# Rotary tables computed once per angle on folded tiles, softplus pinned in its place, and the swaps of rotary halves issued from GpSimd's queue

## The chip, the core and the metric

The kernel runs on one core of a Trainium2 chip. The core has five engines with a queue of instructions each, taken in order: TensorE (PE) multiplies matrices into PSUM, VectorE (DVE) and ScalarE (ACT) work on tiles in SBUF and PSUM, GpSimd (POOL) is a slower helper, and SyncE (SP) mostly issues DMAs. SP, ACT and POOL can each issue DMAs, and all of them run on the same 16 DMA engines. A tile has 128 partitions and some columns. The metric is the device time of one execution in microseconds, as the median of several runs.

## The reference, cut to what matters

The reference is one layer of an encoder trunk over 256 tokens of width 2048, in float32: a norm, one input projection, multi-head latent attention with rotary position encoding beside a bidirectional state-space branch, a gated mix of the two, an output projection, and a gated MLP with a short convolution. What the change touches is the rotary part of the attention and the softplus of the state-space branch:

```
half = QK_ROPE_DIM // 2                                   # 32
inv_freq = ROPE_THETA ** (-jnp.arange(half) / half)
ang = positions[..., None] * inv_freq
cos, sin = jnp.cos(ang), jnp.sin(ang)
apply_rope: [x1 * cos - x2 * sin, x1 * sin + x2 * cos]    # x1, x2: the halves of 64 columns
dt = softplus(dt_raw + dt_bias)
```

There are 32 frequencies and 256 positions, so 8192 different angles. The rotary part of the 16 heads' queries and the one rotary key are turned by them.

## The kernel before

The work is cut into jobs, each one slab of weights (16 blocks of 128x128, two halves of 8) times the activations of all 256 tokens. A slab arrives by SP's queue as `raw`; `split_to` (L139) splits each half into a high part `wh` (ScalarE, L151) and a low part `wl` (VectorE, L152), in rings of five halves, ahead of the products that use them. Products are made in three or two passes (`mm`, `low` in `dense`; L213 to L215 in `quad`), so that the high and low parts together give float32. The first ten jobs are the latent projections of q and kv (jobs 0 to 7), the rotary key (8) and dt (9); then come the gates, R0 and R1 (jobs 11 and 24, the rotary queries of eight heads each), V and QK, the attention, and after it everything else.

The activations are normalized in `emit_n` (L313 to L315, slots 6 to 8): a product with `r_x` (L311), then a split into high and low parts `xHL` (L290, L291). The jobs from 8 on need them.

Side work is hung on jobs by `at(slot, ...)` (L989): it stands ahead of the products of that job in the program. The rotary tables are a generator, `rope_tables` (L323 to L370), of which `rope_steps` takes 4 steps in each job from 5 on. It loads the positions into all 128 partitions of a 256-column tile by one DMA on ACT's queue (L328). Each partition p has the frequency p % 32, so each angle is computed four times, in partitions 32 apart. A chain of VectorE instructions on 128x256 tiles takes the angle modulo a turn (L337, L338, L341), ScalarE makes two Sins (L366, L367), and three more VectorE instructions make the cosine from the half angle's sine and give the sine its sign (L368 to L370).

`swapped` (L372) copies a tile with neighbouring blocks of 32 partitions exchanged, by four DMAs on ACT's queue: once for the rotary key (L511), twice for each of R0 and R1 (L538). `rotate` (L380) multiplies the swapped tile by `sinT`, the tile by `cosT`, and adds; it runs for the key in slot 14 (`kr_rope`) and for R0 and R1 two slots after their jobs, followed by the splits of L552, L553, L517 and L523.

`dt_softplus` (L443) hangs on job 41, `dt_tokens` (L465), which transposes its results on TensorE, on job 46. Its first instruction, an Exp into `nea` (L445), is pinned by `keep_in_program_order`; the Abs behind it (L447) is not.

Only the first weight splits are in an order written out by hand (`manual_schedule`, L1169). All else is ordered by a planner, which gives each engine its instructions in an order of its own by program order and by when it expects an instruction's inputs. On the chip each engine then keeps to that order, and an instruction whose input is late holds up those behind it.

Tiles named by `p1` share 18 buffers of 128x256; `page` tiles share 29 larger ones; `dr` is a pool in DRAM.

Of the kernel before, what the change touches and what calls it, by code (L numbers as in the profile page):

```python
# [8 lines left out]
F32 = mybir.dt.float32  # L9
F32R = mybir.dt.float32r  # L10
I32 = mybir.dt.int32
AF = mybir.ActivationFunctionType
ALU = mybir.AluOpType
AX = mybir.AxisListType

P = 128
S = 256
# [17 lines left out]
C_ID, C_U, C_L, C_INVF, C_SGN = 0, 128, 256, 384, 385  # L35
# [24 lines left out]
def tile_bidir_hybrid_layer(ctx: ExitStack, tc, xT, pos, vec, cst, w_in, w_r, w_v, w_qk, w_oa,  # L60
                            w_os, w_out, w_up, w_dn, out, RAWB=3, HB=5, NPG=29, NP1=18):
    nc = tc.nc
# [5 lines left out]
    dr = ctx.enter_context(tc.tile_pool(name="dr", bufs=1, space=bass.MemoryType.DRAM))  # L68

    act, dve, pe = nc.scalar, nc.vector, nc.tensor  # L70

    def page(shape, dt=F32, name="pg"):
        return pp.tile(shape, dt, tag="pg", bufs=NPG, name=name)

    def p1(shape=(P, S), dt=F32, name="p1"):
        return pp.tile(list(shape), dt, tag="p1", bufs=NP1, name=name)
# [12 lines left out]
    CT = cp.tile([P, NCONST], F32, name="CT")  # L89
# [13 lines left out]
    def vcol(name, i=0):  # L103
        o = VOFF[name] + i
        return V[:, o:o + 1]
# [213 lines left out]


    rot = {}

    def rope_tables():  # L323

        cosT = rot["c"] = p1(name="cosT")
        sinT = rot["s"] = p1(name="sinT")
        pi_ = p1(dt=I32, name="posi")
        nc.scalar.dma_start(pi_, pos.broadcast_to([P, S]))  # L328
        a = p1(name="ang")
        q = p1(name="angq")  # L330
        qh = p1(name="angqh")
        t = p1(name="angt")
        k = p1(name="angk")
        MAGIC = 12582912.0

        def rounded(dst, src, scale):
            yield dve.tensor_scalar(dst, src, scale, MAGIC, ALU.mult, ALU.add)  # L337
            yield dve.tensor_scalar(dst, dst, MAGIC, None, ALU.subtract)  # L338

        def add_scaled(dst, src, c):  # L340
            yield dve.scalar_tensor_tensor(dst, src, c, dst, ALU.mult, ALU.add)  # L341

        def less_turns():
            yield from rounded(k, a, float(np.float32(1.0 / (2 * np.pi))))
            for c in TURN:
                yield from add_scaled(a, k, -c)


        yield dve.tensor_copy(a, pi_)
        yield dve.tensor_scalar(a, a, CT[:, C_INVF:C_INVF + 1], None, ALU.mult)  # L350
        yield from rounded(q, a, 2.0 ** -12)
        yield from add_scaled(a, q, -2.0 ** 12)
        yield from rounded(qh, q, 2.0 ** -10)
        yield from add_scaled(q, qh, -2.0 ** 10)
        yield dve.tensor_scalar(t, qh, TURN22[0], None, ALU.mult)
        yield from add_scaled(t, q, TURN12[0])
        yield from rounded(k, t, 1.0)
        yield dve.tensor_sub(t, t, k)
        yield from add_scaled(t, q, TURN12[1])
        yield from add_scaled(t, qh, TURN22[1])  # L360
        yield from less_turns()
        yield from add_scaled(a, t, 2 * float(np.pi))
        yield from less_turns()
        lim = float(np.nextafter(np.float32(np.pi), np.float32(0)))
        yield dve.tensor_scalar(a, a, lim, -lim, ALU.min, ALU.max)
        act.activation(sinT, a, AF.Sin)  # L366
        yield act.activation(cosT, a, AF.Sin, scale=0.5)  # L367
        yield dve.tensor_mul(cosT, cosT, cosT)  # L368
        yield dve.tensor_scalar(cosT, cosT, -2.0, 1.0, ALU.mult, ALU.add)
        yield dve.tensor_scalar(sinT, sinT, CT[:, C_SGN:C_SGN + 1], None, ALU.mult)  # L370

    def swapped(q, nb):  # L372

        sw = page([P, nb, S], name="sw")
        for i in range(4):
            o = 32 * (i ^ 1)
            nc.scalar.dma_start(sw[o:o + 32], q[32 * i:32 * i + 32])
        return sw

    def rotate(q, sw, nb):  # L380
# [62 lines left out]
    def dt_softplus():  # L443
        v = dts["v"]
        tc.keep_in_program_order(act.activation(nea, vcol("alog"), AF.Exp))  # L445
        e, t, t2, o = p1(name="e"), p1(name="t"), p1(name="t2"), p1(name="o")
        act.activation(e, v, AF.Abs)  # L447
        act.activation(e, e, AF.Exp, scale=-1.0)
        dve.tensor_scalar(t, e, 2.0, None, ALU.add)
        dve.reciprocal(t, t)  # L450
        dve.tensor_mul(t, t, e)
        dve.tensor_mul(t2, t, t)
        n = 9
        dve.tensor_scalar(o, t2, 2.0 / (2 * n + 1), 2.0 / (2 * n - 1), ALU.mult, ALU.add)
        for k in range(n - 2, -1, -1):
            dve.tensor_mul(o, o, t2)
            dve.tensor_scalar(o, o, 2.0 / (2 * k + 1), None, ALU.add)
        dve.tensor_mul(o, o, t)
        dve.scalar_tensor_tensor(o, v, 0.0, o, ALU.max, ALU.add)
        dts["dt"] = o  # L460
        a = p1(name="a")
        dve.tensor_scalar(a, o, nea, -1.0, ALU.mult, ALU.mult)
        dts["a"] = a
# [44 lines left out]
    def kr_evac(ps):  # L508
        t = p1((P, 1, S), name="krf")
        halves_sum(ps, t[:, 0, :])  # L510
        dts["krf"] = (t, swapped(t, 1))  # L511
# [13 lines left out]
    def r_job(i):  # L525
# [3 lines left out]
        def mm(h, n, wh, wl):  # L529
            ps = gpsum([P, 2, S])  # L530
            cell[h] = ps
            for b in range(2):
                for k in range(4):
                    mm3(ps[:, b, :], wh[:, 4 * b + k, :], wl[:, 4 * b + k, :], hi[:, k, :], lo[:, k, :],
                        k == 0, k == 3)
            t = page([P, 2, S], name="rf")
            act.activation(t, ps, AF.Copy)
            cell["f", h] = (t, swapped(t, 2))  # L538
# [450 lines left out]
    def at(slot, fn, *a):  # L989
        late.append((slot, lambda: fn(*a)))  # L990
# [14 lines left out]
    at(10, lat_norm, "kv")  # L1005
    at(13, lat_norm2, "kv", "kvn")
    steps = rope_tables()

    def rope_steps(n):
        for _ in range(n):  # L1010
            next(steps, None)

    for m in range(5, 14):
        at(m, rope_steps, 4 if m < 13 else 99)
    at(14, kr_rope)
    at(41, dt_softplus)
    at(46, dt_tokens)
    at(48, dt_cumsum)
# [67 lines left out]
    for g in range(G):  # L1086
# [9 lines left out]
        e, f = len(jobs) - b, 1  # L1096
# [205 lines left out]
```

## Time and profile before

| what | value |
|---|---|
| median of 3 runs | 1962.73 us (1962.49 to 1963.57) |
| profiled execution: its own time | 1962.68 us |
| its span, first to last instruction | 1960.9 us |
| TensorE busy | 1945.8 us, 99% |
| VectorE busy | 1444.6 us, 74% |
| ScalarE busy | 1205.3 us, 61% |
| GpSimd busy | 0.2 us, 4 instructions |
| mean granted TensorE clock | 0.998 |
| DMA traffic | 379.31 MB, mean 193 GB/s |

The busy times are of one profiled execution. An engine's busy time is the union of its instructions' spans; instructions overlap at their edges, so what one holds its engine for is read from one start to the next. Matmuls are pipelined, so a busy TensorE is not one at its peak. A wait is put down to the semaphore that came last.

### The profile page before, as it was taken

What the parts mean: (1) busy time and instruction counts of PE and PEld (TensorE: products, weight loads), DVE (VectorE), ACT (ScalarE), POOL (GpSimd) and SP (SyncE); (2) the same over time, 40 slices, a digit from 0 to 9 for tenths busy, and PEclk for the clock granted to TensorE, in tenths of its full rate; (3) what the DMA queues carried; (4) which work ended last, traced back from release to release, by engine and by line L of the source; (5) the groups of instructions that cost most, each with busy time, mean ns of one, the idle gap of its engine ahead of it and who ended that gap; (6) DMA issues with size and microseconds to landing.
All of it is one profiled execution on the core that took longest, in us unless ns stands there. A gap on an engine that the chain in (4) does not pass through costs nothing.

```text
span 1960.9 us, 28920 instructions
## 1 busy us (share of the span) xinstructions
PE 1945.8 (99%) x11136; PEld 1707.2 (87%) x11136; DVE 1444.6 (74%) x2349; ACT 1205.3 (61%) x1878; POOL 0.2 (0%) x4
## 2 busy tenths in 40 slices
PE   9999999999999999999999999999999999999997
PEld 8889988888888888888888888888888888888887
DVE  7897744779779789879755566777656777557775
ACT  6566544687887887978644455666435655346553
POOL 0000000000000000000000000000000000000000
PEclk9999999999999999999999999999999999999999
DMA  7554456765665565565666665555555555555543
GB/s 279 179 173 154 137 172 216 251 222 172 215 233 173 198 234 194 194 215 182 205 196 198 200 222 176 190 193 192 181 189 190 194 192 175 194 192 193 188 161 124
DMA packets 93259, 379.31 MB, mean 193 GB/s; under 512 B 10688, under 2 KB 11328, under 8 KB 62912
## 3 DMA queue, kind: packets, MB, share of 16 engines
q1 hardware_dynamic: 91440, 375.09, 56.6%
q10 hardware_dynamic: 1680, 2.37, 0.4%
q8 instruction: 87, 1.43, 0.3%
q14 instruction: 52, 0.43, 0.1%
HBM read 371.91 MB, written 4.33 MB: 192 GB/s over the span
## 4 chain that ended last, share of the span: by engine, by line
PE 95%; DVE 3%; DMA 1%; ACT 1%; issue 0%; ACTq 0%; DVEq 0%; SPq 0%
PE g L178 42%; PE g L185 22%; PE g L214 7%; PE g L213 7%; PE g L215 7%; PE g L159 1%; PE g L157 1%; PE g L158 1%; DVE wl L152 1%; PE s L789 1%; PE s L798 1%; PE s L158 0%; PE s L159 0%; PE s L157 0%; PE s L771 0%; PE s L634 0%
## 5 line engine op out<-in xcount | busy, mean ns | idle before, releaser
L152 DVE TENSOR_TENSOR wl<-raw,wh 128x1024 fp32r<-128x1024 f32 (+1 forms) x670 | 802.7, 1209 | 328.1 <-ACT wh L151 181.3
L151 ACT ACTIVATE wh<-raw 128x1024 fp32r<-128x1024 f32 (+1 forms) x670 | 698.9, 1047 | 546.6 <-PE g L178 352.0
L178 PE MATMUL g<-xHL,wh 128*128 128x512 f32 x1424 | 341.7, 392 | 1.3 <-DVE xHL L291 1.1
L178 PE MATMUL g<-hHL,wh 128*128 128x512 f32 x1360 | 324.8, 391 | 0.0
L178 PEld LDWEIGHTS g<-xHL,wh 128*128 128x128 f32 x1424 | 262.4, 188 | 53.6 <-DVE xHL L291 1.5
L178 PEld LDWEIGHTS g<-hHL,wh 128*128 128x128 f32 x1360 | 249.8, 188 | 48.3
L185 PEld LDWEIGHTS g<-xHL,wl 128*128 128x128 f32 x1424 | 182.6, 191 | 7.0
L185 PE MATMUL g<-xHL,wl 128*128 128x256 f32 x1424 | 184.9, 283 | 0.0
L185 PEld LDWEIGHTS g<-hHL,wl 128*128 128x128 f32 x1360 | 174.3, 191 | 6.6
L185 PE MATMUL g<-hHL,wl 128*128 128x256 f32 x1360 | 176.4, 283 | 0.0
L178 PE MATMUL g<-aHL,wh 128*128 128x512 f32 x692 | 166.6, 391 | 0.1
L910 DVE SCALAR_TENSOR_TENSOR uc<-u,V,uc 128x255 f32<-128x255 f32 x176 | 85.3, 485 | 88.4 <-ACT uc L908 85.3
L178 PEld LDWEIGHTS g<-aHL,wh 128*128 128x128 f32 x692 | 126.9, 188 | 25.6 <-DVE aHL L928 1.3
L213 PE MATMUL g<-wh,yHL 128*128 128x512 f32 x256 | 100.1, 391 | 0.0
L214 PE MATMUL g<-wl,xHL 128*128 128x512 f32 x256 | 100.0, 391 | 0.0
L213 PE MATMUL g<-wh,xHL 128*128 128x512 f32 x256 | 100.0, 391 | 0.0
L215 PE MATMUL g<-wh,yHL 128*128 128x512 f32 x256 | 99.7, 389 | 0.0
L215 PE MATMUL g<-wh,xHL 128*128 128x512 f32 x256 | 99.6, 389 | 0.0
L214 PE MATMUL g<-wl,yHL 128*128 128x512 f32 x256 | 99.6, 389 | 0.0
L185 PEld LDWEIGHTS g<-aHL,wl 128*128 128x128 f32 x692 | 89.2, 191 | 3.6
L185 PE MATMUL g<-aHL,wl 128*128 128x256 f32 x692 | 90.4, 283 | 0.0
L684 DVE SCALAR_TENSOR_TENSOR xs<-cu,V,xs 128x254 f32<-128x254 f32 (+1 forms) x128 | 59.0, 479 | 0.2
(298 smaller groups left out, 2534.1 us busy)
## 6 DMA issues: line engine op xcount, KB each, us to landing
raw<-in_w_in SPq DMA_DIRECT2D x88, 1024.0 KB, 4.9
raw<-in_w_up SPq DMA_DIRECT2D x88, 1024.0 KB, 4.8
raw<-in_w_in SPq DMA_DIRECT2D x128, 256.0 KB, 3.9
raw<-in_w_os SPq DMA_DIRECT2D x128, 256.0 KB, 3.6
raw<-in_w_dn SPq DMA_DIRECT2D x32, 1024.0 KB, 5.0
raw<-in_w_oa SPq DMA_DIRECT2D x64, 256.0 KB, 3.9
FB<-acsD SPq DMA_DIRECT2D x32, 512.0 KB, 7.4
raw<-in_w_out SPq DMA_DIRECT2D x14, 1024.0 KB, 5.0
```

Source lines behind the costliest of these rows:

```text
L151: act.activation(vh, r, AF.Copy)
L152: dve.tensor_sub(vl, r, f32(vh))
L157: pe.matmul(ps, lhsT=wH, rhs=xH, start=first, stop=False)
L158: pe.matmul(ps, lhsT=wH, rhs=xL, start=False, stop=False)
L159: pe.matmul(ps, lhsT=wL, rhs=xH, start=False, stop=last)
L178: pe.matmul(ps, lhsT=wh[:, b, :], rhs=x, start=k == 0, stop=False)
L185: pe.matmul(cell["ps"][:, 0, :], lhsT=wl[:, b, :], rhs=get(k)[:, 0, :], start=False, stop=k == ktot - 1)
L213: pe.matmul(ps, lhsT=x[:, 0, ts], rhs=wH[:, kk, :], start=k == 0, stop=False)
L214: pe.matmul(ps, lhsT=x[:, 0, ts], rhs=wL[:, kk, :], start=False, stop=False)
L215: pe.matmul(ps, lhsT=x[:, 1, ts], rhs=wH[:, kk, :], start=False, stop=k == kt - 1)
L684: dve.scalar_tensor_tensor(o[:, a], u[:, b], vcol("cw", k * 48 + cb), o[:, a], ALU.mult, ALU.add)
L910: dve.scalar_tensor_tensor(o[:, a], u[:, b], vcol("fcw", k * 88 + cb), o[:, a], ALU.mult, ALU.add)
```

## The change

The positions are loaded folded: partition block c (32 partitions) of a 64-column tile holds positions 64c to 64c+63, by four DMAs on ACT's queue. Each angle is then computed once, on 128x64 tiles, which are slices of one tile `ang`; sine and cosine lie side by side in `tr`. Four DMAs from GpSimd's queue store the pair to DRAM (`rotD`, 32 x 2 x 256), and eight load it back, four for the cosine and four for the sine, each into 32 partitions of a 128x256 tile. The sign is applied after that, on the spread tile. `rope_steps` takes 8 steps in each job from 5 on, not 4. `swapped` issues its DMAs from GpSimd's queue. The Abs of the softplus is pinned to its place in the program.

```
     rot = {}
+    rotD = dr.tile([32, 2, S], F32, name="rotD")
     def rope_tables():
-        cosT = rot["c"] = p1(name="cosT")
-        sinT = rot["s"] = p1(name="sinT")
-        pi_ = p1(dt=I32, name="posi")
-        nc.scalar.dma_start(pi_, pos.broadcast_to([P, S]))
-        a = p1(name="ang")
-        q = p1(name="angq")
-        qh = p1(name="angqh")
-        t = p1(name="angt")
-        k = p1(name="angk")
+        pi_ = p1((P, 64), I32, name="posi")
+        w = p1((P, 4, 64), name="ang")
+        a, q, qh, t = (w[:, i, :] for i in range(4))
+        k = p1((P, 64), name="angk")
+        tr = p1((P, 2, 64), name="trig")
+        cosT, sinT = tr[:, 0, :], tr[:, 1, :]
+        for c in range(4):
+            nc.scalar.dma_start(pi_[32 * c:32 * c + 32], pos[:, 64 * c:64 * c + 64].broadcast_to([32, 64]))
...
         yield dve.tensor_scalar(cosT, cosT, -2.0, 1.0, ALU.mult, ALU.add)
-        yield dve.tensor_scalar(sinT, sinT, CT[:, C_SGN:C_SGN + 1], None, ALU.mult)
+        for c in range(4):
+            nc.gpsimd.dma_start(rotD[:, :, 64 * c:64 * c + 64], tr[32 * c:32 * c + 32])
+        for i, nm in enumerate("cs"):
+            rot[nm] = p1(name="rot")
+            for c in range(4):
+                nc.gpsimd.dma_start(rot[nm][32 * c:32 * c + 32], rotD[:, i, :])
+        yield dve.tensor_scalar(rot["s"], rot["s"], CT[:, C_SGN:C_SGN + 1], None, ALU.mult)
     def swapped(q, nb):
...
-            nc.scalar.dma_start(sw[o:o + 32], q[32 * i:32 * i + 32])
+            nc.gpsimd.dma_start(sw[o:o + 32], q[32 * i:32 * i + 32])
...
-        act.activation(e, v, AF.Abs)
+        tc.keep_in_program_order(act.activation(e, v, AF.Abs))
...
-    for m in range(5, 14):
-        at(m, rope_steps, 4 if m < 13 else 99)
+    for m in range(5, 11):
+        at(m, rope_steps, 8 if m < 10 else 99)
```

## Rows read from the trace of the kernel before

**Rows 1.** Head of the page: span, busy us of each engine (share) xinstructions.
```profile
span 1960.9 us, 28920 instructions
...
PE 1945.8 (99%) x11136; PEld 1707.2 (87%) x11136; DVE 1444.6 (74%) x2349; ACT 1205.3 (61%) x1878; POOL 0.2 (0%) x4
```

**Rows 2.** TensorE's waits: line, releaser: us in total, times, longest us.
```profile
PE g L178 <- DVE xHL L291: 1.1, 1, 1.1
PE g L159 <- DVE wl L152: 1.1, 1, 1.1
...
PE s L269 <- DVE dg L268: 0.9, 1, 0.9
...
PE g L178 <- DVE cu L238: 0.2, 1, 0.2
```

**Rows 3.** Timeline of TensorE: start us, us, what [idle before <-releaser].
```profile
61.58 3.04 PE L178 MATMUL g<-xHL,wh 128*128 128x512 f32 x12 [1.10 <-DVE xHL L291]
...
101.53 0.50 PE L574 MATMUL g<-wl,latH 128*128 128x512 f32 x1 [0.28 <-DVE wl L152]
...
105.71 0.38 PE L159 MATMUL g<-latH,wl 128*128 128x256 f32 x1 [1.10 <-DVE wl L152]
```

**Rows 4.** Windows, 45 to 82 us: length, busy us of each engine, clock.
```profile
45.00:82.00 37.00, 35.90 (x215) 31.68 (x215) 36.02 (x76) 19.77 (x33) 0.00 (x0) 1.00 0.54 174
```

**Rows 5.** VectorE's waits from 40 to 130 us, columns as in rows 2.
```profile
DVE sw L382 <- DMA sw<-rf: 2.4, 1, 2.4
DVE sinT L370 <- ACT sinT L366: 1.9, 1, 1.9
DVE xw L314 <- ACT r_x L311: 1.3, 1, 1.3
...
DVE ang L349 <- DMA posi<-in_pos: 0.7, 1, 0.7
```

**Rows 6.** Timeline of ScalarE and its queue, 40 to 110 us.
```profile
41.51 0.34 ACTq L328 DMA_DIRECT2D posi<-in_pos  x1
41.80 0.36 ACT L311 ACTIVATE r_x<-s 128x256 f32<-128x256 f32 x1
...
82.39 1.28 ACT L366 ACT_TABLE_LOAD   x1 [1.32 <-issue]
...
105.53 0.41 ACT L447 ACTIVATE e<-dtv 128x256 f32<-128x256 f32 x1
```

**Rows 7.** Tile sw: ns min/median/max, first and last start; then landing us.
```profile
L377 ACTq DMA_DIRECT2D sw<-rf x16: 514/602/752, 81.1 to 174.1; - x16
...
DMA to landing us min/median/max: 2.0/4.4/7.2
```

**Rows 8.** Timeline of VectorE, 45 to 80 us, columns as in rows 3.
```profile
49.14 0.42 DVE L341 SCALAR_TENSOR_TENSOR ang<-angq,ang 128x256 f32<-128x256 f32 x1
49.47 0.28 DVE L337 TENSOR_SCALAR angqh<-angq 128x256 f32<-128x256 f32 x1
49.67 1.22 DVE L152 TENSOR_TENSOR wl<-raw,wh 128x1024 fp32r<-128x1024 f32 x1
...
73.58 0.15 DVE L411 TENSOR_TENSOR u<-u,rtok 128x2 f32<-128x2 f32 x1
73.65 1.22 DVE L152 TENSOR_TENSOR wl<-raw,wh 128x1024 fp32r<-128x1024 f32 x1
```

**Rows 9.** DMA issues through DRAM: count, KB each, median us to landing.
```profile
FB<-acsD SPq DMA_DIRECT2D x32, 512.0 KB, 7.4
...
acsD<-row SPq DMA_DIRECT2D x2, 64.0 KB, 3.0
```

**Rows 10.** Line L445, the pinned Exp of softplus, columns as in rows 7.
```profile
L445 ACT ACTIVATE nea<-V x1: 184/184/184, 280.9 to 280.9; 128x1 f32<-128x1 f32 x1
```

**Rows 11.** Line L469, TensorE's transposes of the softplus results.
```profile
L469 PE MATMUL s<-CT,o x2: 271/272/272, 309.6 to 309.7; 128*128 128x128 f32 x2
```

**Rows 12.** Windows, 250 to 300 us, columns as in rows 4.
```profile
250.00:300.00 50.00, 50.00 (x230) 41.67 (x229) 24.35 (x26) 23.20 (x30) 0.00 (x0) 1.00 0.53 171
```

## The prediction

> **What bounds the kernel now.** I read the page's busy list first: TensorE works 1945.8 us of a 1960.9 us span, and GpSimd does next to nothing (4 instructions, 0.2 us) [rows 1]. A change to VectorE, ScalarE and a DMA queue can give back only what TensorE waits for. The list of TensorE's own waits says how much that is [rows 2]: beside those at the start and in the final norm (`dg` is the longest), which nothing here touches, there are three in the stretch where the rotary tables are made. One of 1.1 us ends at 61.58 us, for `xHL` (the normalized activations, L291); one of 0.3 us ends at 101.53 us and one of 1.1 us at 105.71 us, both for `wl` (the low weight half, L152) [rows 2, 3]. That is 2.5 us together, all for VectorE. The only other one in the body is 0.2 us.
>
> Then the question is what makes VectorE late. It is busy 36.0 of the 37 us from 45 to 82 us [rows 4]. Its longest waits [rows 5] are 2.4 us for the swap of R0's rotary halves (`sw<-rf`), 1.9 us for the sine, 1.3 us for `r_x`, 0.7 us for the positions. It takes instructions in order, so each also holds up the weight splits behind it. The first two, 4.3 us, fall where the Sin's table is loaded (82.39 us) and R0's swaps are under way (from 81.1 us) [rows 6, 7], and 1.4 us of them came through to TensorE some 12 us later; splits made ahead covered the other 2.9 us.
>
> **The folded tables.** From the code: the generator has 31 steps, 30 of them VectorE instructions (14 with two tensor inputs, 16 with one) and the two Sin activations as one step. At 256 columns a two-input step holds VectorE for 0.33 us (49.14 to 49.47) and a one-input step for 0.20 us (49.47 to 49.67); a 128x2 instruction holds it for 0.07 us (73.58 to 73.65) [rows 8]. Straight between these, 64 columns cost 0.07 + 0.26/4 = 0.135 us and 0.07 + 0.13/4 = 0.10 us. The bounds are 0.07 for either (width is all) and the old prices (width is nothing). Saved: 14 x 0.195 + 15 x 0.10 = 2.7 + 1.5 = 4.2 us of VectorE (the sign multiply stays at 256 columns); bounds 0 and 14 x 0.26 + 15 x 0.13 = 5.6.
>
> Where it is saved matters. Steps now go 8 to a job from job 5, not 4. Before the second pair of `emit_n` (slot 8), 12 steps ran: 3 x 0.33 + 9 x 0.20 = 2.8 us. Now 24 run: 11 x 0.135 + 13 x 0.10 = 2.8 us. So in front of the wait that ends at 61.58 us the fold gives nothing. The whole 4.2 us come after it, ahead of the second and third wait.
>
> **The positions.** One issue of 0.34 us on ScalarE's queue becomes four, right ahead of `r_x` (41.51, then 41.80) [rows 6], for which VectorE already waits 1.3 us [rows 5]. That is 3 x 0.34 = 1.0 us if they stand in the same place, 0 if they fill an earlier gap of ScalarE. Queued behind: `r_x` on ScalarE; for that wait the `emit_n` products, and for those TensorE at 61.58 us. I take the middle, +0.5 us on TensorE.
>
> **The Sin.** It now runs in job 8, ahead of the square root of the second latent norm (slot 10), so one more table load of 1.28 us [rows 6] comes into ScalarE, off the path: that norm is used at slot 13, three jobs later. If that cover were gone it would cost its 1.28 us. VectorE's 1.9 us wait for the sine [rows 5] goes, or turns into the wait for the spread, next.
>
> **The spread.** Four stores of the folded pair to DRAM and eight loads back, all on GpSimd's queue; the loads wait for the stores. No DMA of GpSimd's is in the trace, so I bound it with the other queues. Issue: 0.34 us (the positions) [rows 6] to 0.75 us (slowest swap), 0.60 us in the middle; landing 2.0 to 7.2, median 4.4 us [rows 7]. A store to DRAM and a load from it took 3.0 and 7.4 us elsewhere [rows 9]. Low: 4 x 0.34 + 2.0 + 8 x 0.34 + 2.0 = 8.1 us. High: 4 x 0.75 + 7.2 + 8 x 0.75 + 7.4 = 23.6 us. I take 4 x 0.6 + 4.4 + 8 x 0.6 + 4.4 = 16 us, because the swaps are the nearest rows in size and time. The folded pair is ready at about 69.5 us: job 8 has its products at 61.6 us [rows 3], then come seven dependent steps among other work (4 us), a table load of 1.28 us and four short instructions. So the tables are there at 78 to 93 us, most likely at 85.5 us. Before, they were there at about 85 us (the table load at 82.39 [rows 6], then two activations and three steps). The early start pays for the detour and no more.
>
> By the Trainium skill ("DMA: Bandwidth & Descriptors", section "Specifications") a transfer from GpSimd's path starts after about 1 us, against about 0.6 us from the other two. By that figure the two hops would end 0.8 us later (an estimate); no run here shows it yet.
>
> **The swaps.** ScalarE loses the issues, 20 at 0.60 us [rows 7]: 2.4 us for the rotary key at 67 us, 4.8 us for R0 from 81 us on, the same for R1. The latent norm's scale and weight copies stood behind them; I count no gain of its own, since ScalarE is behind VectorE in none of TensorE's waits [rows 2]. The same DMAs leave from GpSimd's queue, in order behind the spread. R0's first half is there at 81.1 us; by my middle price the last load of the spread is issued at 69.5 + 2.4 + 4.4 + 4.8 = 81.1 us, so R0's swaps are not held up and land near 90 us as before. At the high price the queue is free only at 69.5 + 3.0 + 7.2 + 6.0 = 85.7 us, and they land 4.6 us later. R1's (the last issued at 174.1 us [rows 7]) meet an empty queue and cost nothing.
>
> **Softplus.** The Abs ran at 105.5 us, drawn far forward, while the pinned Exp in the line above it ran at 280.9 us [rows 6, 10]. Now the whole chain, 22 VectorE instructions, runs from about 281 us: at 0.33 us some 7 us, twice that if each waits for the one before. The transposes that need it start at 309.6 us [rows 11], and VectorE is busy 24.4 of 50 us there [rows 12]: 28 us of cover, cost nothing. What it frees after 105 us is not waited for either [rows 2]; it is room to catch up in.
>
> **Sum.** First wait: +0.5. Second and third, 1.4 us: the fold's 4.2 us and the sine's 1.9 us outweigh them, -1.4; late next is the swap, which stays. Net -0.9 us on the profiled execution: span 1960.0. That execution took 1962.68 us, 1.8 us around its span, and stands 0.05 us under the median of the runs. Forecast: 1961.8 us.
>
> **Rivals.** *The late queue (slower).* The sign multiply, or the product with `sw`, stands in VectorE's order where its transfer is expected early, and GpSimd's queue is late. At the high price the tables come 7.6 us after 85.5 us. VectorE stands for it with the weight splits behind it; the 4.2 us of the fold are used up first, and what is over falls on TensorE one for one, on top of the 1.4 us that then stay and the +0.5: 7.6 - 4.2 + 0.5 = +3.9, so 1966.6 us. Against it: 4.3 us of such standing came down to 1.4 us before. For it: the wait for `sw` is already VectorE's longest [rows 5], and 24 issues now share one queue between 69 and 90 us. It decides from about 0.75 us an issue or 7 us a landing. Chance 0.17.
>
> The Trainium skill ("SBUF — State Buffer", section "Who interferes with whom") says that GpSimd cannot write a DMA's descriptors while VectorE runs in a mode that takes both its ports, as one-input instructions can. Such an instruction is 0.20 us apart from the next here [rows 8], so 24 issues would be held up by 4.8 us at most, an estimate; it is one more way into this rival, and no run here shows it yet.
>
> *Only moved.* The swap still lands at 90 us, and the rotation and the splits of its result are still due after it, so the 1.4 us stay, and the positions cost 0.5 to 1.0 us: 1963.4 us. For it: the savings lie before 90 us, and the ring of five halves cannot bank more than it holds. In effect the change would not do what it says. Chance 0.27.
>
> *All three waits go.* The positions are issued in an earlier gap and the denser steps fit between other work: -2.5 us, 1960.2 us. Against it: 2.8 us of steps before slot 8 either way. Chance 0.12.
>
> **How the numbers follow.** Forecast 0.44 (own range 1961.0 to 1962.6 us), moved 0.27, late queue 0.17, all gone 0.12. A difference of 0.2%, 3.9 us, is about what a measurement of this kernel can tell from no change. Faster than that needs more than all of the 2.5 us; I keep 0.03 of the last case for a reordering that I can't see. Slower 0.17, same 0.80. The range goes from all waits gone to just short of the late queue's price: 1959.9 to 1966.2 us.
>
> **What would show it.** Right: TensorE's waits for `wl` near 101 to 106 us gone, the one for `xHL` near 61 us between 1.1 and 2.1 us, folded steps 0.10 to 0.14 us apart, no swap issues on ScalarE, the Abs near 281 us and no wait at the transposes. Wrong: VectorE standing over 4 us before the sign multiply or the product with `sw` and then waits for `wl` above 1.4 us; a spread shorter than 8.1 or longer than 23.6 us; a new wait after 130 us; a fall of the granted clock where TensorE stood.

## The result and the profile after

The changed kernel takes 1965.95 us (median of 20 runs, 1964.23 to 1967.16) against 1962.32 us (1961.68 to 1963.57): the ratio is 1.0018, with a 95% interval of 1.0011 to 1.0025. It is 3.6 us slower, where 0.9 us faster was forecast, and the time lies inside the stated range.

The profiled execution is one of the quicker ones: 1964.54 us, span 1962.7. Head of its page:

```profile
span 1962.7 us, 28976 instructions
...
PE 1945.2 (99%) x11136; PEld 1706.7 (87%) x11136; DVE 1441.9 (73%) x2349; ACT 1206.2 (61%) x1879; POOL 16.1 (1%) x36
```

TensorE's work is what it was [rows 1]; GpSimd has 32 instructions more. TensorE's waits (line, releaser: us in total, times, longest us):

```profile
PE g L158 <- DVE latL L432: 3.1, 1, 3.1
...
PE g L214 <- DVE wl L152: 0.6, 1, 0.6
PE g L157 <- ACT gate L667: 0.5, 1, 0.5
```

The 1.1 us for `xHL` and both waits for `wl` of [rows 2, 3] are gone. A single wait of 3.1 us has come, for `latL` (L432), the low half of the normalized q latents, which R0's products need. With 0.6 and 0.5 us of new small ones that is 4.2 us against 2.5, so +1.7 us; the span is 1.8 us longer. (The waits at the start and in the final norm are left out on both sides. They are 0.5 us longer here, so such an account holds to about half a microsecond.) Why `latL` is late stands in the timeline of VectorE (start us, us, what, [idle before <-releaser]):

```profile
78.22 0.42 DVE L447 TENSOR_TENSOR dtv<-dtv,g 128x256 f32<-128x256 f32 x1
82.20 0.41 DVE L377 TENSOR_SCALAR rot<-rot,CT 128x256 f32<-128x256 f32 x1 [3.56 <-DMA rot<-rotD]
82.53 0.20 DVE L417 TENSOR_TENSOR u<-s,rtok 128x1 f32<-128x1 f32 x2
82.66 1.21 DVE L152 TENSOR_TENSOR wl<-raw,wh 128x1024 fp32r<-128x1024 f32 x1
83.79 1.21 DVE L432 TENSOR_TENSOR latL<-q,latH 128x1024 fp32r<-128x1024 f32 x1
84.92 0.15 DVE L418 TENSOR_TENSOR u<-u,rtok 128x2 f32<-128x2 f32 x1
```

From 78.6 to 82.2 us VectorE stands for the spread (`rot<-rotD`) at the sign multiply, L377. Three more instructions follow it, and then `latL`, whose input `latH` ScalarE had made at 79.4 us. In the kernel before, the sign multiply (L370 there) came 9 us after `latL`:

```profile
74.82 1.22 DVE L425 TENSOR_TENSOR latL<-q,latH 128x1024 fp32r<-128x1024 f32 x1
...
84.14 0.35 DVE L370 TENSOR_SCALAR sinT<-sinT,CT 128x256 f32<-128x256 f32 x1 [1.89 <-ACT sinT L366]
```

VectorE's waits from 40 to 130 us, those that answer to [rows 5]:

```profile
DVE rot L377 <- DMA rot<-rotD: 3.6, 1, 3.6
...
DVE xw L314 <- ACT r_x L311: 1.3, 1, 1.3
...
DVE sw L389 <- DMA sw<-rf: 0.8, 1, 0.8
```

The waits for the sine (1.9), for the positions (0.7) and most of that for the swap (2.4, now 0.8) are gone, and one of 3.6 us has come. The queue that it waits for, GpSimd's timeline:

```profile
69.11 2.22 POOL L372 DMA_DIRECT2D rotD<-trig  x4 [68.66 <-ACT wh L151]
76.23 3.93 POOL L376 DMA_DIRECT2D rot<-rotD  x8 [4.90 <-DMA rotD<-trig]
81.50 1.96 POOL L384 DMA_DIRECT2D sw<-krf  x4 [1.34 <-issue]
89.81 1.96 POOL L384 DMA_DIRECT2D sw<-rf  x4 [6.35 <-ACT rf L544]
```

### The profile page after: what moved, and what is told of

It reads as the page before. It is cut to its first block, busy times and chain, and to the rows that moved or that the text cites. A ratio compares the mean times of both kernels' runs of the same rounds, so it can differ in the third digit from the quotient of the medians.

```text
span 1962.7 us, 28976 instructions
## 1 busy us (share of the span) xinstructions
PE 1945.2 (99%) x11136; PEld 1706.7 (87%) x11136; DVE 1441.9 (73%) x2349; ACT 1206.2 (61%) x1879; POOL 16.1 (1%) x36
## 4 chain that ended last, share of the span: by engine, by line
PE 93%; DVE 1%; ACT 1%; DMA 0%; issue 0%; DVEq 0%; ACTq 0%
PE g L178 41%; PE g L185 21%; PE g L213 7%; PE g L214 7%; PE g L215 7%; PE g L159 1%; PE g L157 1%; PE g L158 1%; PE s L796 1%; PE s L805 1%; PE s L158 0%; PE s L159 0%; PE s L157 0%; PE s L778 0%; PE s L641 0%; PE g L580 0%
```

## The experiments

The theory (A): the sign multiply waits for a transfer, VectorE keeps its order, and so `latL` behind it is late. The rivals: (B) the swaps on GpSimd's queue are late; (C) something beside the waits, such as the granted clock or GpSimd's transfers as such. Each kernel ran against the kernel before on the same chip (there 1962.1 to 1962.3 us).

**The changed kernel again.** No edit.

> The changed kernel once more, to see what its times scatter with. Theory A (the sign multiply on the spread table stands in VectorE's order ahead of latL, and waits for the spread): TensorE again stands 2.5 to 4 us near 82 to 85 us for latL, median 1965 to 1966.5 us, and the slower executions have a longer wait there. Theory C (beside that wait, about half of the 3.6 us comes from a lower granted clock in some executions): the times fall with the mean granted clock, about 1 us for each 0.0005, and the kernel before doesn't show that scatter. If A alone holds, the clock is the same in all.

Measured: 1966.1 us (1965.27 to 1967.95). In this profiled execution (1966.75 us) TensorE waited 4.1 us for `latL`, and something followed. Windows of it (length, busy us of each engine, then granted clock, DMA share, GB/s), and below the same windows of the first profiled execution, where the wait was 3.1 us:

```profile
80.00:86.00 6.00, 2.02 (x10) 1.34 (x8) 2.72 (x6) 2.34 (x2) 3.70 (x8) 1.00 0.34 65
86.00:91.00 5.00, 4.92 (x28) 4.92 (x29) 3.05 (x10) 0.97 (x3) 0.00 (x0) 0.66 0.52 197
```

```profile
86.00:91.00 5.00, 5.00 (x45) 5.00 (x44) 3.25 (x9) 1.80 (x3) 1.19 (x3) 1.00 0.42 170
```

After the wait of 4.1 us the mean granted clock from 86 to 91 us is 0.66: for 3.4 of the five microseconds it was at 1.2 GHz and not 2.4, so 1.7 us of work were lost. With the wait of 3.1 us the clock stayed at 1.00. Waits and clock account for the time: 4.1 + 0.4 + 0.4 - 2.5 = 2.4 us, and 1.7, make 4.1 us, and this span (1965.0) exceeds that of the kernel before (1960.9) by as much. That it fits to the tenth is chance, since the waits left out above are 0.5 us longer here too. Over the 20 runs of the first set the times go with the mean clock: the five at 0.998 took 1964.2 to 1965.0 us, the ten at 0.997 took 1965.3 to 1967.0 us, the five at 0.996 took 1966.0 to 1967.2 us. In this execution the longer wait cost twice. That part of theory C is right; that GpSimd's transfers as such cost anything is not needed for the sum.

**The sign multiply at slot 13.** The order alone.

```
-        yield dve.tensor_scalar(rot["s"], rot["s"], CT[:, C_SGN:C_SGN + 1], None, ALU.mult)
+    def rope_sign():
+        dve.tensor_scalar(rot["s"], rot["s"], CT[:, C_SGN:C_SGN + 1], None, ALU.mult)
...
+    at(13, rope_sign)
     at(14, kr_rope)
```

> The sign multiply on the spread table is hung on job 13 instead of ending the generator in job 8, so that it stands behind latL in VectorE's order. It still waits for the same transfers. Theory A: TensorE's wait for latL goes, as with the folded minus sine, 1961 to 1963.5 us, though VectorE may still stand there for the spread. Rival B: no difference from the changed kernel, 1965 to 1966 us. If only the length of VectorE's wait mattered and not what stands behind it, 1964 to 1966 us.

Measured: 1961.58 us (1960.90 to 1964.38), 4.5 us under the changed kernel and level with the kernel before (ratio 0.9998, 0.9989 to 1.0007). The built order differs from the changed kernel's in the sign multiply, the order of the key's two rotation products and the place of a reciprocal on VectorE, in the place of one matmul, and nowhere else. VectorE's timeline, then its wait and TensorE's:

```profile
79.95 1.22 DVE L434 TENSOR_TENSOR latL<-q,latH 128x1024 fp32r<-128x1024 f32 x1
...
85.84 0.35 DVE L379 TENSOR_SCALAR rot<-rot,CT 128x256 f32<-128x256 f32 x1 [2.98 <-DMA rot<-rotD]
```

```profile
DVE rot L379 <- DMA rot<-rotD: 3.0, 1, 3.0
```

```profile
PE s L269 <- DVE dg L268: 1.9, 2, 1.1
...
PE g L214 <- DVE wl L152: 0.5, 1, 0.5
```

VectorE still stands 3.0 us for the spread, almost as long as before, but `latL` went ahead; TensorE pays 1.1 us for `dg`, which now stands behind it (the other 0.9 of the 1.9 is in the final norm), and the clock stays up. Theory A holds: what costs is not the wait but what it stands in front of.

**Four loads, not eight.**

```
+    rotT = cp.tile([P, 2, S], F32, name="rotT")
...
-            rot[nm] = p1(name="rot")
-            for c in range(4):
-                nc.gpsimd.dma_start(rot[nm][32 * c:32 * c + 32], rotD[:, i, :])
+            rot[nm] = rotT[:, i, :]
+        for c in range(4):
+            nc.gpsimd.dma_start(rotT[32 * c:32 * c + 32], rotD)
```

> The spread loads sine and cosine together: four DMAs into one tile of 128x2x256 and not eight, so four issues of 0.5 us fewer on GpSimd's queue, and the tables are there some 2 us earlier, at about 80 us. In this build the planner also puts the sign multiply behind latL by itself. Theory A: no wait of TensorE for latL, VectorE's wait for the spread 0 to 1.5 us, median 1960 to 1962 us. If it is the number of GpSimd's transfers that costs, about a sixth of the 3.6 us comes back: 1965 to 1966 us.

Measured: 1961.47 us (1960.59 to 1961.82). The time came as theory A has it, the reason only in part: the tables were no earlier.

```profile
74.25 1.23 DVE L433 TENSOR_TENSOR latL<-q,latH 128x1024 fp32r<-128x1024 f32 x1 [0.62 <-ACT latH L432]
...
82.78 0.35 DVE L378 TENSOR_SCALAR rotT<-rotT,CT 128x256 f32<-128x256 f32 x1 [4.25 <-DMA rotT<-rotD]
```

VectorE stood 4.3 us, longer than in the changed kernel, with `latL` already done (the planner had put it first), and TensorE's only waits there were 0.6 and 0.3 us for `wl`. Four issues fewer did not shorten the spread: from 69.2 us, the first store's issue, to 82.8 us are 13.6 us, of which the issues of stores and loads take 4.2 and the landings most of the rest. It is no clean test of their number, since each load carries twice the bytes and lands later (4.1 us in the median, against 3.6 in the changed kernel).

**Minus sine on the folded tile.** No VectorE instruction between the spread and the rotations; `tr` and `rotD` are one table larger.

```
...
+        yield dve.tensor_scalar(tr[:, 2, :], sinT, -1.0, None, ALU.mult)
...
+                nc.gpsimd.dma_start(rot[nm][32 * c:32 * c + 32], rotD[:, i if i == 0 else 2 - c % 2, :])
-        yield dve.tensor_scalar(rot["s"], rot["s"], CT[:, C_SGN:C_SGN + 1], None, ALU.mult)
```

> Minus sine is made on the folded tile (128x64) and spread as a third table, so no VectorE instruction needs the spread before the rotations. Nothing else changes: GpSimd still issues 4 + 8 table DMAs and 20 swaps. Theory A: the 3.6 us wait of VectorE and the 3.1 us wait of TensorE for latL go, median 1961 to 1963 us, at or under the kernel before. Rival B (R0's swaps on GpSimd's queue are what is late): TensorE still waits 3 us or more between 82 and 107 us, 1965 to 1966 us. Theory C in the form that GpSimd's transfers themselves lower the clock: 1963.5 to 1964.5 us.

Measured: 1967.25 us (1963.78 to 1968.65), a miss. The wait for `latL` did go, and another came:

```profile
PE g L157 <- ACT gate L667: 4.3, 1, 4.3
...
PE g L214 <- DVE wl L152: 0.5, 1, 0.5
```

```profile
DVE sw L389 <- DMA sw<-rf: 3.7, 2, 1.9
DVE sw L389 <- DMA sw<-krf: 1.9, 1, 1.9
```

VectorE now stands three times at the products with `sw`, 5.6 us in all. ScalarE's timeline tells what was behind the last of these:

```profile
104.71 1.28 ACT L559 ACTIVATE rp<-rf 64x512 fp32r<-64x512 f32 x2 [3.44 <-DVE rf L391]
106.00 1.28 ACT L667 ACT_TABLE_LOAD   x1
107.30 1.09 ACT L667 ACTIVATE gate<-g 128x512 f32<-128x512 f32 x2
```

`rp` (L559) waited 3.4 us for VectorE, the table load and the gates' tanh (L667) stood behind `rp`, and TensorE needed the PSUM tiles that the tanh frees. The granted clock then fell (a mean of 0.72 from 106 to 112 us), 1.7 us more. So rival B has a share in this build: a late swap costs as much, if what waits for it stands in front of something needed. In the changed kernel the same chain cost 0.5 us.

**The swaps back on ScalarE's queue**, in the changed kernel.

```
-            nc.gpsimd.dma_start(sw[o:o + 32], q[32 * i:32 * i + 32])
+            nc.scalar.dma_start(sw[o:o + 32], q[32 * i:32 * i + 32])
```

> The changed kernel with the 20 swap DMAs back on ScalarE's queue; the spread stays on GpSimd's. Theory A: the sign multiply still waits for the spread (the swaps stand behind it in GpSimd's queue and cannot delay it), TensorE still stands about 3 us, 1964.5 to 1966.5 us. Rival B: the swaps are early again, 1962 to 1963 us.

Measured: 1969.86 us (1968.75 to 1971.27), worse than either theory had it. The wait for `latL` stayed, as A says, and a second one came; B, that the swaps' queue is to blame, falls for the changed kernel.

```profile
PE g L158 <- DVE latL L432: 3.4, 1, 3.4
PE g L581 <- DVE wl L152: 3.3, 1, 3.3
```

The clock fell after both, as the windows (columns as above) show:

```profile
86.00:91.00 5.00, 4.90 (x28) 4.90 (x29) 2.86 (x9) 0.48 (x1) 0.00 (x0) 0.66 0.54 197
106.00:112.00 6.00, 5.59 (x17) 4.43 (x18) 5.82 (x10) 5.63 (x8) 0.00 (x0) 0.72 0.45 167
```

That is 1.7 us of work lost each time. With 3.4 + 3.3 + 0.4 - 2.5 = 4.6 us of waits it makes 8.0 us; the span (1968.6) is 7.7 us longer than that of the kernel before. Which instruction makes the second wait was not tested.

**The same in the version with four loads.**

> The version with four loads (sign multiply behind latL) with the 20 swaps back on ScalarE's queue: what the move of the swaps is worth once nothing waits for the spread ahead of latL. If the issues on ScalarE's queue hold up the latent norm and the weight copies, a wait for wl or latL of 1 to 3 us comes back, 1962.5 to 1965 us. If the move is worth nothing by itself, 1961 to 1962 us.

Measured: 1960.61 us (1960.23 to 1961.00), 0.9 us under four loads with the swaps on GpSimd's queue. With `latL` in front, the move of the swaps is worth nothing here; that what it gave above (1969.9 against 1966.1 us) came from the bad order is inferred from the two pairs. This version differs from the pin alone (1961.98 us, below) in the folded tables and their spread only. It is 1.4 us faster, 1.2 if each is taken against the kernel before beside it, and the ranges do not overlap: once `latL` stands in front, the fold is worth about the 1.4 us that the sum had for it.

**The swaps alone**, in the kernel before.

> The kernel before with only the 20 swap DMAs moved to GpSimd's queue. Theory A: no sign multiply waits for a transfer here, so it is no slower; ScalarE gets its 12 us of issues back, the latent norm is earlier, and part of the 1.4 us wait for wl goes: 1960.5 to 1962.5 us. Rival B (swaps from GpSimd's queue land late): VectorE's wait for sw grows from 2.4 us to over 4 us and the time is 1963.5 us or more.

Measured: 1963.79 us (1963.06 to 1964.38), 1.5 us slower by the medians, though the interval of the ratio (0.9999 to 1.0016) just takes in no change. The waits for `wl` went, as A has it, but not the time; the time is as B has it, but VectorE's wait for `sw` was 2.1 us, not over 4. New waits of TensorE came at the attention:

```profile
PE g L573 <- DVE qk L597: 1.6, 1, 1.6
...
PE g L213 <- DVE vl L581: 0.4, 1, 0.4
PE s L634 <- DVE p L626: 0.4, 1, 0.4
```

**The pin alone**, in the kernel before, and **the changed kernel without it.**

> The kernel before with only the Abs of the softplus pinned. All theories: the softplus runs from about 281 us with no wait of TensorE at the transposes, 1962.0 to 1962.7 us. If the freed time of VectorE at 105 to 145 us were worth anything to TensorE, under 1961.5 us.

> The changed kernel without the pin of the Abs. Theory A: the wait for latL stays at 3 to 4 us, since nothing of the softplus stands ahead of 105 us, 1965 to 1967 us. If the pin had disturbed the planner's order around 80 us and so made the wait, 1961 to 1963 us.

Measured: 1961.98 us (1961.26 to 1962.95), no difference that can be told; and 1966.57 us (1964.95 to 1967.54), with a wait of 3.9 us for `latL` in its profile. The pin neither makes nor mends the loss.

**Swaps and pin**, in the kernel before: no folding, no spread.

> The kernel before with the swaps on GpSimd's queue and the Abs pinned; the tables stay unfolded, nothing is spread. With the swaps alone TensorE's waits for wl at 101 to 106 us went, but new ones of 1.6, 0.4 and 0.4 us came at the attention, where VectorE also does the softplus. If the softplus makes those, they go with the pin: 1960.5 to 1961.8 us. If the later or denser swaps make them, 1963 to 1964 us as with the swaps alone.

Measured: 1960.29 us (1959.82 to 1960.96), ratio 0.9991 (0.9982 to 1.0000); the slowest of its 11 runs is under the quickest of the 20 beside it (1961.31). Windows from 110 to 130 us, with the swaps alone and with swaps and pin:

```profile
110.00:130.00 20.00, 17.64 (x109) 15.51 (x110) 19.62 (x40) 7.74 (x14) 0.00 (x0) 1.00 0.53 186
```

```profile
110.00:130.00 20.00, 20.00 (x130) 18.15 (x129) 14.87 (x24) 10.91 (x20) 0.00 (x0) 1.00 0.54 184
```

Without the pin VectorE is full there (19.6 of 20 us) and TensorE busy for 17.6; with it VectorE has 5 us to spare and TensorE none. So the softplus made those waits, and the two parts are worth 1.9 us together where the one alone costs 1.5 and the other gives 0.3, which can't be told from nothing. This is the lowest median of all that ran, 0.09% under the kernel before; the version with four loads and the swaps on ScalarE's queue is 0.3 us behind, with a range that overlaps.

## Why the prediction was wrong

- **The bound** was read rightly: what moved is TensorE's waits in this stretch, and the granted clock with them. That a difference of 0.2% "is about what a measurement of this kernel can tell from no change" was wrong: the interval of the measured 0.18% is 0.14% wide and clear of no change.
- **The folded tables**: right. Two-input steps stand 0.14 us apart and one-input steps 0.10 (forecast 0.135 and 0.10), by the timeline of VectorE around 49 us:

```profile
49.32 0.22 DVE L342 SCALAR_TENSOR_TENSOR ang<-ang 128x64 f32<-128x64 f32 x1
49.46 0.19 DVE L338 TENSOR_SCALAR ang<-ang 128x64 f32<-128x64 f32 x1
49.56 0.69 DVE L291 TENSOR_TENSOR xHL<-xw,xHL 128x512 fp32r<-128x512 f32 x1
```

- **The positions**: the size was wrong. +0.5 us was forecast for the first wait; it went from 1.1 us for `xHL` to 0.6 us for `wl`. Only one of the four issues stood ahead of `r_x`. The other three took 0.84 us each on average behind it; ScalarE stood 2.3 us for them ahead of an `xHL` half, and no wait of TensorE came of it:

```profile
41.40 0.34 ACTq L334 DMA_DIRECT2D posi<-in_pos  x1
41.69 0.36 ACT L311 ACTIVATE r_x<-s 128x256 f32<-128x256 f32 x1
41.77 2.51 ACTq L334 DMA_DIRECT2D posi<-in_pos  x3
44.33 1.16 ACT L290 ACTIVATE xHL<-xw 128x512 fp32r<-128x512 f32 x2 [2.28 <-issue]
```

- **The spread**: it was quicker than its middle price. From the first store's issue at 69.1 us to the sign multiply at 82.2 us are 13.1 us, within 8.1 to 23.6, against 16 forecast; an issue takes 0.5 us on GpSimd's queue.
- **The swaps**: "I count no gain of its own, since ScalarE is behind VectorE in none of TensorE's waits" put at nothing a term that was not nothing. In the kernel before, the chain that ends in the wait at 105.71 us runs through ScalarE's queue: its issues of R0's swap, with the Sin's table load among them, then the landing, then VectorE:

```profile
81.10 0.51 ACTq L377
...
82.39 0.61 ACT L366
...
83.04 6.80 DMA sw<-rf
...
89.96 0.69 DVE sw L382
```

With the swaps alone moved, that product starts at 87.23 us, and the 1.4 us for `wl` are gone without any fold.
- **The step that failed** is "the early start pays for the detour and no more", and the sum built on it ("-1.4; late next is the swap"). It compared when the tables are there with when they were there before. What counts is where their first user stands in VectorE's order. Before, the multiply followed the Sin, behind `latL`; afterwards the program asks for it in job 8, the planner put it ahead of `latL` with three instructions between, and tables that came 3 us before the time forecast were still 3.6 us late for that place. So the 1.4 us went as the sum has it, and a new wait of TensorE came that it has nothing for: 3.1 us in one execution and 4.1 in another, with a fall of the clock after the longer. The slot-13 run, with next to nothing but that order changed, took the loss away.
- **The rival of the late queue** had the right place and the wrong condition. It was to decide "from about 0.75 us an issue or 7 us a landing"; the issues took 0.5 us and the swaps landed after 3.7 us in the median, and it came about all the same. That its 1966.6 us lies near the measured 1965.95 is luck, since it was priced for tables 7.6 us later than forecast and they came 3 us earlier; and the stated range holds the measured time only because it reaches to just short of that price. Its price also set the 4.2 us of the fold against VectorE's standing. They could not help, because `latL` itself, no split made ahead, stood behind.
- **Left out** altogether: that a wait of TensorE can be followed by a stretch at the lower clock, 1.7 of the 4.1 us that the changed kernel lost in its second profiled execution. I had named a fall of the clock as a sign of error and given it no price.
- **Softplus**: right by itself (Abs at 282.5 us, no wait at the transposes), and wrong in "not waited for": with the swaps moved, its 10 us of VectorE (7 forecast; a reciprocal alone takes 1.75) are waited for.
- By the Trainium skill ("SBUF — State Buffer", section "Who interferes with whom") VectorE's two-port instructions keep GpSimd from writing descriptors. No run here shows it, and none tests it well: the 16 issues for R0 and R1 took 496 to 498 ns, but beside nearly all of them VectorE stood idle or ran instructions of other kinds. One issue for the key's swap ran beside the one-input sign multiply and took 496 ns as well. By the Trainium skill ("DMA: Bandwidth & Descriptors", section "Specifications") a transfer from GpSimd's path starts after about 1 us, against about 0.6 us from the other two. No run here sets that apart: the swaps landed after 3.7 us in the median, after 4.4 from ScalarE's queue [rows 7], each beside other traffic.

```profile
L384 POOL DMA_DIRECT2D sw<-rf x16: 496/496/498, 89.8 to 175.9; - x16
...
DMA to landing us min/median/max: 1.7/3.7/5.6
```

Open: why the planner put the sign multiply where it did. The runs show the order it gave and what that cost, not its reckoning. And that the clock falls with such a wait was seen in several traces; no run was made to find out when it does.

## What to carry to other kernels

When work is moved so that a result comes by a slower way, do not ask only whether it comes as early as it did; ask where its first user now stands in its engine's queue, and what stands behind it. A wait of 4 us on VectorE cost next to nothing where only banked work was behind it, and 3 to 4 us of TensorE, mostly with a fall of the clock, where the next products' operand was. And test the parts of a change in pairs: here one part cost 1.5 us alone, by the medians, and gained with its partner.

## What the runs showed of the hardware that was not expected

The granted clock was at its lower level for 3.4 us after TensorE had stood 4.1 us (the changed kernel run again), 3.4 us and 3.3 us (the swaps back on ScalarE's queue) and 4.3 us (minus sine on the folded tile). In the changed kernel without the pin it fell within a wait of 3.9 us, some 2 us before its end, and was low for 6.8 us (0.86 as the mean from 80 to 85 us, 0.66 from 85 to 93 us). After the wait of 3.1 us it did not fall. An issue of the same swaps took 0.50 us on GpSimd's queue and 0.60 us on ScalarE's (medians) [rows 7]; of the folded positions on ScalarE's queue the first took 0.34 us and the other three 0.84 us on average.
